# A hybrid attention layer on one core: attention buffers taken in order of release, two more buffers each for the stick-breaking weights, and their products with the values one unit later

## The chip, the cores and the metric

One core of one Trainium2 chip runs the whole layer. The metric is device time in microseconds. The kernel before takes 2918.4 us, the median of three runs (2916.21 to 2920.43). Names of engines follow the profile: PE is the matrix engine, PEld its weight load, DVE, ACT and POOL are the vector, scalar and general engines, SP is the engine that issues nearly all DMAs. Each engine works through its own instructions strictly in the order in which they were written.

## The reference, cut to what matters

Input and output are 2048 tokens by 1024 channels. One projection feeds two kinds of attention heads whose outputs are concatenated, projected and added; a SwiGLU feed-forward part follows.

```python
def stick_breaking_attention(q, k, v):          # 8 heads x 64
    ...
        z = jnp.einsum('bhqd,bhkd->bhqk', q[:, :, start:end], k[:, :, :end]).astype(jnp.float32) * scale
        log_beta = jax.nn.log_sigmoid(z)
        log_1m = jnp.where(past, jax.nn.log_sigmoid(-z), 0.0)
        acc = lax.cumsum(log_1m, axis=3, reverse=True) - log_1m
        w = jnp.where(past, jnp.exp(log_beta + acc), 0.0)
        outs.append(jnp.einsum('bhqk,bhkd->bhqd', w.astype(v.dtype), v[:, :, :end]))
    ...
def differential_attention(q, k, v, lam):       # 4 heads, two 64-wide q/k maps each
    ...
        p = jax.nn.softmax(jnp.where(causal, s, -jnp.inf), axis=-1)
        a = p[:, :, 0] - lam * p[:, :, 1]
        outs.append(jnp.einsum('bhqk,bhkd->bhqd', a.astype(v.dtype), v[:, :, :end]))
```

## The kernel before, in words

The program has four stretches: the first norm and projections, the stick-breaking heads in four groups of two heads (groups 0 to 3), the differential heads in four groups (4 to 7), and output projection and feed-forward. Every float32 product is done as three half-precision products, of a high part and a low part.

A group of stick-breaking heads is swept in *units*. A unit is one block of 128 queries (a = 0 or 1) against one piece of up to 512 keys, for both heads. Two units with the same keys, a = 0 and a = 1, make a *step*; a group has 20 steps, so there are 160 units in all. The sweep of a unit, `unit_sb`, is this:

- `scores` (PE): z = q k into PSUM. Two places in PSUM are used in turn, so the scores of unit u wait until DVE has read those of unit u-2.
- `main`: three sigmoids on ACT (L756 into `be`, L757 into `gp`, L758 within PSUM), two scans on DVE that form the running product (L761), a multiplication on DVE (L764), then on DVE the low part `wl` of the unit three back (L790, run by `clock.run("low")`), the carry from the step before (L769, or L767 where there is none), and a multiplication on POOL (L772).
- two units later `high` (ACT, L785): the high half `wh` of the weights; SP then issues a DMA that transposes it into `wt`.
- three units later `low` (DVE, L790): the low half `wl`, and its transposing DMA into a second `wt`.
- for a = 1, five units later `values` (PE): the transposed weights of the whole step, `wt`, times v.

The order is set by hand. `clock.at(d, fn, kind)` hangs work on the unit d units ahead; in each unit the loop over the plan runs the kinds "ev", "", main, "mid" and the rest in that order, then issues the scores of the unit after it, and then fills PE with projections of coming heads as long as PE's planned work is short of a goal. `values` has the kind "", so on PE it stands ahead of that unit's scores and filling. In many units there is nothing to fill with.

Buffers come from pools with a fixed number each: seven `pp` (L278) for `gp`, `be` and, in the other stretches, for input rows, normed rows and softmax weights; four `wh` (L281); four `wt` (L289, L780), two per step. Which buffer of a pool a new tile gets is the pool's choice when the program is built, and a write to it waits for the last reader of the tile that had it. Some of these choices fall on a buffer that was let go only lately: in group 1 tile `gp_4576` of unit 72 lies at the address of `be_4337` of unit 68, whose last reader is a `wl` that DVE runs in the unit just ahead (71). The room of the pools `csp`, `stp` and `rtp` is for the rotation of the differential heads' q and k; it is first written late in group 3.

Of the kernel before, what the change touches and what calls it, by code (L numbers as in the profile page):

```python
# [7 lines left out]
F32 = mybir.dt.float32  # L8
# [56 lines left out]
def hybrid_layer_kernel(  # L65
# [159 lines left out]
    with ExitStack() as actx:  # L225
        ac = actx.enter_context(tc.tile_pool(name="ac", bufs=1))
        OWN, NWT = (3,), 4
# [4 lines left out]
        csp = actx.enter_context(tc.tile_pool(name="csp", bufs=1))  # L232
        wtp = actx.enter_context(tc.tile_pool(name="wtp", bufs=NWT))
        stp = actx.enter_context(tc.tile_pool(name="stp", bufs=2))
        rtp = actx.enter_context(tc.tile_pool(name="rtp", bufs=1))
        onp = actx.enter_context(tc.tile_pool(name="onp", bufs=2))
        mxp = actx.enter_context(tc.tile_pool(name="mxp", bufs=2))
        psp = actx.enter_context(tc.tile_pool(name="psp", bufs=1, space=PSUM))
# [39 lines left out]
        def ptile(name):  # L278
            return ppp.tile([128, 1028], F32, tag="pp", name=name)

        def htile(name):  # L281
            return whp.tile([128, 1024], F16, tag="wh", name=name)

        wts = []

        def transposed(wh, w):

            if not wts:
                wt = wtp.tile([128, 2, 1024], F16, tag="wt", name="wt")  # L289
                wts.extend((wt[:, 0], wt[:, 1]))  # L290
            wt = wts.pop(0)[:, 0:w]
            nc.sync.dma_start_transpose(out=wt.rearrange("p (b q) -> p b q", q=128), in_=wh)
            return wt

        lam_t = rtp.tile([128, 1024], F32, tag="rt", name="lam_t")
# [267 lines left out]
        def project_diff(c, g):  # L563
# [10 lines left out]
            st = stp.tile([128, 2, 4, 2, 64], F32, tag="st", name="st")  # L574
# [43 lines left out]
            def squares():  # L618
                r["cs"] = csp.tile([128, 2, 4, 32], F32, tag="cs", name="cs")
# [3 lines left out]
                r["rt"] = rtp.tile([128, 1024], F32, tag="rt", name="rt")  # L623
# [87 lines left out]

        def units_sb(g):
# [7 lines left out]
        def unit_sb(g, s, c, a, cx, step):  # L720
# [27 lines left out]
            def main():  # L748


                z, sc = u["z"], scl[g]
                if a == 0:
                    step["gp"] = ptile("gp").rearrange("p (a h n) -> p a h n", a=2, h=2)
# [41 lines left out]
                if a == 1:  # L795
                    clock.at(5, values, "")
# [935 lines left out]
```

## Time and profile before

| | us |
|---|---|
| median of three runs | 2918.4 |
| the profiled execution: its time | 2919.95 |
| the profiled execution: its span | 2918.2 |
| busy in the span: PE, DVE, ACT, POOL | 2559.5, 2321.2, 1537.5, 1460.1 |
| groups 0 to 2 of the stick-breaking heads | 90 to 593 |
| group 3, and the turn to the differential heads | 593 to 815 |
| differential heads | 815 to 1506 |
| the rest of output projection, feed-forward | 1506 to 2918 |

The limits of the stretches were read from the times at which their lines first and last run, and are good to a unit or so. A row of a timeline is start, duration, engine, line, operation, what is written and read, and in brackets how long the engine had stood idle ahead of it and what ended that. A row of a table of waits is the waiting engine and line, what it waited for, and the microseconds in total, the number of times and the longest. A wait matters when the waiting engine is one on which the end depends; the chain of waits tells which those were.

### The profile page before, as it was taken

The page shows a single profiled execution, that of the slowest core. Times are in us where ns is not written, and L with a number is a line of the kernel's source. Part 1 is how long each engine was busy: PE and PEld are TensorE (multiplying, and loading weights), DVE is VectorE, ACT ScalarE, POOL GpSimd, SP SyncE. Part 2 cuts the span into 40 slices and gives each one's busy share as a digit, 9 for nine tenths or more (in the row PEclk, how much of TensorE's full clock was granted, in tenths as well). Part 3 has the DMA queues.
Part 4 walks back from the last instruction along what each step waited for, and adds up shares of the span by engine and source line. Part 5 has one row for each costly group of instructions (what it writes and reads, how often), then busy time and mean ns, then how long its engine had stood idle before and what let it go on. Part 6 is the DMA issues. An engine that isn't in the chain of part 4 may idle for free.

```text
span 2918.2 us, 50458 instructions
## 1 busy us (share of the span) xinstructions
PE 2559.5 (88%) x19628; PEld 1475.6 (51%) x19628; DVE 2321.2 (80%) x3639; ACT 1537.5 (53%) x2587; POOL 1460.1 (50%) x1131
## 2 busy tenths in 40 slices
PE   6868878888687787776998899999999999999999
PEld 4435444446576676665763344444444444444444
DVE  7787878878898899899747788889877776776776
ACT  5777777877555555555415454544443343343332
POOL 1344444546667577576115456555445454445442
PEclk9979989889798899988999999999999999999999
DMA  4466776776745565667866312221126422112111
GB/s 157 83 129 119 131 131 114 140 127 124 130 74 96 94 106 100 127 121 135 188 155 139 106 65 103 96 80 62 44 87 132 135 94 73 44 44 87 44 44 72
DMA packets 734240, 301.55 MB, mean 103 GB/s; under 512 B 618672, under 2 KB 713264, under 8 KB 734000
## 3 DMA queue, kind: packets, MB, share of 16 engines
q1 hardware_dynamic: 733856, 298.30, 45.6%
q8 instruction: 153, 2.51, 0.4%
q14 instruction: 87, 0.71, 0.1%
q0 software_dynamic: 144, 0.03, 0.0%
HBM read 127.34 MB, written 28.31 MB: 53 GB/s over the span
## 4 chain that ended last, share of the span: by engine, by line
PE 48%; DVE 22%; ACT 9%; DMA 7%; POOL 6%; issue 6%; SPq 1%; DVEq 0%; ACTq 0%; POOLq 0%
PE pw L167 33%; PE psum L167 15%; DMA wt<-wl 3%; DVE mx L178 2%; DVE fs L1316 2%; DVE wl L790 2%; DVE acc_a L1589 2%; DVE gp L761 2%; ACT be L756 2%; DVE pt L178 1%; ACT gp L757 1%; DVE hh L1368 1%; DVE be L764 1%; ACT wh L785 1%; ACT psum L758 1%
## 5 line engine op out<-in xcount | busy, mean ns | idle before, releaser
L167 PE MATMUL pw<-t,fs 128*128 128x512 f16 x3696 | 808.5, 381 | 13.3 <-ACT fs L1315 3.8
L167 PEld LDWEIGHTS <-fs 128*128 128x128 f16 x3696 | 360.5, 98 | 452.4 <-issue 13.9
L772 POOL TENSOR_TENSOR be<-be,gp 128x1024 f32<-128x1024 f32 (+1 forms) x160 | 323.1, 2019 | 363.6 <-DVE gp L769 177.7
L167 PE MATMUL pw<-acc_b,at 128*128 128x512 f16 x2112 | 465.5, 380 | 17.2 <-DVE cg L1514 6.3
L167 PE MATMUL psum<-k,q 64*128 64x512 f16 (+4 forms) x1600 | 293.0, 383 | 131.9 <-ACT pt L874 79.8
L167 PE MATMUL psum<-ws,h_hi 128*128 128x128 f16 x4096 | 378.9, 225 | 17.3 <-ACT psum L948 10.8
L167 PE MATMUL psum<-ws,h_lo 128*128 128x128 f16 x2048 | 367.7, 224 | 0.0
L167 PEld LDWEIGHTS <-h_hi 128*128 128x128 f16 x4096 | 328.8, 101 | 47.5 <-issue 35.4
L167 PEld LDWEIGHTS <-at 128*128 128x128 f16 x2112 | 206.1, 98 | 268.7 <-issue 24.9
L1517 POOL TENSOR_TENSOR cg<-cg,cu 128x512 f32<-128x512 f32 x88 | 111.9, 1272 | 360.9 <-ACT cg L1516 341.1
L1589 DVE SCALAR_TENSOR_TENSOR acc_a<-pw,isd,acc_a 128x512 f32<-128x512 f32 x352 | 248.6, 744 | 49.9 <-PE pw L167 49.5
L761 DVE TENSOR_TENSOR_SCAN gp<-gp,psum 128x256 f32<-128x256 f32 (+1 forms) x320 | 196.4, 655 | 114.8 <-ACT psum L758 112.9
L1315 ACT ACTIVATE fs<-acc_b,fst 128x512 f16<-128x512 f32 x264 | 175.9, 713 | 211.1 <-POOL acc_b L1304 145.1
L1316 DVE SCALAR_TENSOR_TENSOR fs<-acc_b,fst,fs 128x512 f16<-128x512 f32 x264 | 248.2, 980 | 34.0 <-ACT fs L1315 33.9
L1506 POOL TENSOR_TENSOR sc<-sc 128x512 f32<-128x512 f32 x132 | 219.3, 1678 | 88.9 <-ACT sc L1500 88.9
L167 PEld LDWEIGHTS <-q 64*128 64x128 f16 (+1 forms) x1600 | 95.8, 100 | 239.2 <-issue 116.4
L167 PE MATMUL psum<-wt,v 128*64 128x256 f16 x1728 | 138.8, 308 | 84.8 <-DMA wt<-wl 74.4
L1500 ACT COPY sc<-pw 128x512 f32<-128x512 f32 x176 | 100.1, 580 | 211.4 <-PE pw L167 185.2
L167 PEld LDWEIGHTS <-h_lo 128*128 128x128 f16 x2048 | 206.5, 101 | 0.0
L874 ACT ACTIVATE pt<-psum,nb,ds_sc 128x1024 f32<-128x1024 f32 (+4 forms) x192 | 182.8, 952 | 21.6 <-DVE pt L178 8.3
L178 DVE TENSOR_REDUCE mx<-psum 128x1 f32<-128x1024 f32 (+4 forms) x192 | 173.6, 904 | 22.3 <-PE psum L167 21.6
L790 DVE TENSOR_TENSOR wl<-be,wh 128x1024 f16<-128x1024 f32 (+1 forms) x160 | 186.8, 1168 | 0.9 <-DMA wt<-wl 0.8
(224 smaller groups left out, 4596.3 us busy)
## 6 DMA issues: line engine op xcount, KB each, us to landing
acc_b<-in_w_gate_dram SPq DMA_DIRECT2D x22, 1024.0 KB, 5.2
acc_b<-in_w_up_dram SPq DMA_DIRECT2D x22, 1024.0 KB, 7.5
acc_b<-in_w_down_dram SPq DMA_DIRECT2D x22, 1024.0 KB, 9.4
raw<-in_w_in_dram SPq DMA_DIRECT2D x24, 512.0 KB, 4.5
xt<-in_x_dram SPq DMA_DIRECT2D x16, 512.0 KB, 5.5
raw<-in_w_o_dram SPq DMA_DIRECT2D x16, 512.0 KB, 4.0
mt<-mix_d SPq DMA_DIRECT2D x32, 256.0 KB, 3.4
out_dram<-acc_a SPq DMA_DIRECT2D x16, 512.0 KB, 2.6
```

The costliest lines, as they stand in the source:

```text
L167: nc.tensor.matmul(ps, lhsT=lhsT, rhs=rhs, start=start, stop=stop)
L178: fn(*a, **k)
L761: nc.vector.tensor_tensor_scan(ga, ga, z[:, h, P:W][:, ::-1], 2.0 ** 14 if diag else cx[a][:, h, 0:1], ALU.mult, ALU.mult)
L772: nc.gpsimd.tensor_mul(b4, b4, gp[:, :, 1:P + 1].rearrange("p h (r n) -> p h r n", r=1).to_broadcast([128, 2, 2, P]))
L790: nc.vector.tensor_sub(wl, b2, u["wh"])
L874: nc.scalar.activation(pt, u["z"][:, 0:e - b], AF.Exp, scale=ds_sc, bias=nb[:, m:m + 1], accum_out=su[:, jj:jj + 1])
L1315: nc.scalar.activation(w[:, m, 0:4], src, AF.Copy, scale=sw)
L1316: nc.vector.scalar_tensor_tensor(w[:, m, 4:8], src, sw, w[:, m, 0:4], ALU.mult, ALU.subtract)
L1500: nc.scalar.copy(s[m], y[m])
L1506: nc.gpsimd.tensor_add(s[m], s[m], y[m])
L1517: nc.gpsimd.tensor_mul(g, g, u)
L1589: nc.vector.scalar_tensor_tensor(acc[:, i, hs], ps, pr.isd, acc[:, i, hs], ALU.mult, ALU.add)
```

## The change

Three things change, all in the attention part.

1. The pools of `pp`, `wh` and `wt` become rings: buffers made once, a list of the free ones in the order in which the program let them go, and a new tile takes the one that has been free longest (`take`, `give`). `gp` gets two `pp` buffers of its own, used in turn, for as long as the stick-breaking heads last; the other five serve `be`.
2. Two more `wh` and two more `wt` lie in the room of `csp`, `stp` and `rtp`. From the first unit of group 3 on they are taken only if nothing else is free, and `settle` gives the room over to the rotation when all four are free.
3. `values` runs six units after its step in groups 0 to 2. In group 3 it stays at five.

```diff
-        ppp = actx.enter_context(tc.tile_pool(name="ppp", bufs=7))
-        whp = actx.enter_context(tc.tile_pool(name="whp", bufs=4))
...
-        wtp = actx.enter_context(tc.tile_pool(name="wtp", bufs=NWT))
...
+        class Ring:
...
+            def __init__(self, name, n, shape, dt, pool=rgp):
+                self.all = [pool.tile(shape, dt, tag=f"{name}{i}", name=name) for i in range(n)]
+                self.free = list(self.all)
+                self.last = []
+
+            def take(self):
+                keep = [not any(t is l for l in self.last) for t in self.free]
+                return self.free.pop(keep.index(True) if True in keep else 0)
+
+            def give(self, t):
+                self.free.append(t)
+
+        pps = Ring("pp", 7, [128, 1028], F32)
+        whs = Ring("wh", 4, [128, 1024], F16)
+
+        wts = Ring("wt", 4, [128, 2, 1024], F16)
+
+        more_x = ExitStack()
+        mop = more_x.enter_context(tc.tile_pool(name="mop", bufs=1))
+        extra = [(ring, Ring(name, 2, shape, F16, mop).all)
+                 for ring, name, shape in ((whs, "wh", [128, 1024]), (wts, "wt", [128, 2, 1024]))]
+        for ring, tiles in extra:
+            ring.free.extend(tiles)
...
+        def settle():
+
+            if not pools:
+                if not all(any(t is f for f in ring.free) for ring, tiles in extra for t in tiles):
+                    return False
+                for ring, tiles in extra:
+                    ring.free = [f for f in ring.free if not any(t is f for t in tiles)]
+                more_x.close()
+                for name, bufs in (("csp", 1), ("stp", 2), ("rtp", 1)):
+                    pools[name] = actx.enter_context(tc.tile_pool(name=name, bufs=bufs))
+            return True
+
+        def retire():
+
+            for ring, tiles in extra:
+                ring.last = tiles
...
+            while not settle():
+                yield END
             while staged[0] == 2:
                 yield END
...
+                if not gps:
+                    gps.extend((pps.take(), pps.take()))
                 if a == 0:
-                    step["gp"] = ptile("gp").rearrange("p (a h n) -> p a h n", a=2, h=2)
-                gp = step["gp"][:, a]
-                be = ptile("be")[:, 0:2 * W].rearrange("p (h n) -> p h n", h=2)
+                    gps.reverse()
+                if g == SBP - 1 and s == 0:
+                    retire()
+                gp = gps[0].rearrange("p (a h n) -> p a h n", a=2, h=2)[:, a]
+                bt = pps.take()
+                be = bt[:, 0:2 * W].rearrange("p (h n) -> p h n", h=2)
...
                 def high():
-                    wh = u["wh"] = htile("wh")[:, 0:n]
-                    nc.scalar.copy(wh, b2)
-                    turned(wh, 0)
+                    wh = u["wh"] = whs.take()
+                    nc.scalar.copy(wh[:, 0:n], b2)
+                    turned(wh[:, 0:n], 0)
 
                 def low():
-                    wl = htile("wl")[:, 0:n]
-                    nc.vector.tensor_sub(wl, b2, u["wh"])
-                    turned(wl, 1)
+                    wl = whs.take()
+                    nc.vector.tensor_sub(wl[:, 0:n], b2, u["wh"][:, 0:n])
+                    turned(wl[:, 0:n], 1)
+                    whs.give(u["wh"])
+                    whs.give(wl)
+                    pps.give(bt)
...
                 if a == 1:
-                    clock.at(5, values, "")
+                    clock.at(6 if g < SBP - 1 else 5, values, "")
...
+                for y in range(2):
+                    wts.give(step[y])
                 if c == 0:
                     clock.at(2, store, "")
```

The input rows, the softmax weights and the weight halves of the differential heads take and give back in the same way; a `pp` tile of the first softmax map goes back when the two maps are mixed, the other when its low part is formed.

What the built programs then hold, at two places. The first is ACT in group 1, two steps without a diagonal, before and then after (`pp_124` and `pp_127` are the two `gp` buffers now, the other `pp` are `be`; the old names carry a number of their own for each tile). What an instruction waits for stands in brackets, by engine or DMA lane.

```order
L756 ACTIVATE be_4577<-psum_122,gsc_137 128x1024 [waits PE_49]
L757 ACTIVATE gp_4576<-psum_122,gsc_137 128x2x256 [waits DVE_49]
L758 ACTIVATE psum_122<-psum_122,gsc_137 128x2x256 [waits Activation_49]
L785 CAST wh_4589<-be_4438 128x1024 [waits DMAHW1_49,Pool_49]
L756 ACTIVATE be_4625<-psum_122,gsc_137 128x1024 [waits DVE_49,PE_49]
L757 ACTIVATE gp_4576<-psum_122,gsc_137 128x2x256
```

```order
L802 ACTIVATE pp_126<-psum_107,gsc_122 128x1024 [waits DVE_49,PE_49]
L803 ACTIVATE pp_127<-psum_107,gsc_122 128x2x256 [waits DVE_49]
L804 ACTIVATE psum_107<-psum_107,gsc_122 128x2x256 [waits Activation_49]
L831 CAST wh_132<-pp_125 128x1024 [waits DMAHW7_49,Pool_49]
L802 ACTIVATE pp_129<-psum_107,gsc_122 128x1024 [waits DVE_49,PE_49]
L803 ACTIVATE pp_127<-psum_107,gsc_122 128x2x256 [waits DVE_49]
```

Both write `gp` after a wait for DVE, but for another instruction: before, for L790 in the unit just ahead; now for L815 (the carry, old L769) two units back. The wait of `be` for DVE now stands in most units, and is for L836 (the low part, old L790) that DVE runs two units back.

The second place is SP in group 1, the transposing DMAs of two steps, before and then after.

```order
L781 DMA_TRANSPOSE wt_5722<-wh_5720 128x8x128 [waits DMAHW5_49,DMAHW7_49,PE_49,Activation_49]
L781 DMA_TRANSPOSE wt_5787<-wl_5785 128x8x128 [waits DMAHW6_49,DVE_49,PE_49]
L781 DMA_TRANSPOSE wt_5722<-wh_5791 128x8x128 [waits Activation_49]
L781 DMA_TRANSPOSE wt_5787<-wl_5873 128x8x128 [waits DMAHW0_49,DVE_49]
L781 DMA_TRANSPOSE wt_5882<-wh_5880 128x8x128 [waits DMAHW2_49,DMAHW1_49,DMAHW4_49,PE_49,Activation_49]
```

```order
L827 DMA_TRANSPOSE wt_143<-wh_132 128x8x128 [waits DMAHW5_49,PE_49,Activation_49]
L827 DMA_TRANSPOSE wt_144<-wh_133 128x8x128 [waits DMAHW6_49,DVE_49]
L827 DMA_TRANSPOSE wt_143<-wh_141 128x8x128 [waits DMAHW7_49,Activation_49]
L827 DMA_TRANSPOSE wt_144<-wh_142 128x8x128 [waits DMAHW0_49,DVE_49]
L827 DMA_TRANSPOSE wt_134<-wh_130 128x8x128 [waits DMAHW1_49,PE_49,Activation_49]
```

The number and order of the DMAs stay, apart from the stores of results (`mix_d`), which move with `values`. The first DMA of a step waits for PE before and now, but three steps instead of two lie between two uses of a `wt`, and three units instead of two between two uses of a `wh`. On PE the products with the values move behind one more unit's scores and filling; the rest of PE's order is the same but for single pieces of filling.

More of the change, by code (lines that the diff above doesn't have):

```diff
@@ L293, in transposed @@
+        def retire():
+            for ring, tiles in extra:
+                ring.last = tiles
+        halves_free = []
+        def transposed(wh, w):
+            if not halves_free:
+                t = wts.take()
+                halves_free.extend((t[:, 0], t[:, 1]))
+            wt = halves_free.pop(0)
+            nc.sync.dma_start_transpose(
+                out=wt[:, 0:w].rearrange("p (b q) -> p b q", q=128), in_=wh)
             return wt
-        lam_t = rtp.tile([128, 1024], F32, tag="rt", name="lam_t")
+        lam_t = whs.free[-1].bitcast(F32)
@@ L872, in main @@
                                          scale=nds_sc, bias=lnk)
-                pt = ptile("pt")[:, 0:e - b]
+                while gps:
+                    pps.give(gps.pop())
+                cx["t", m, j] = pps.take()
+                pt = cx["t", m, j][:, 0:e - b]
                 nc.scalar.activation(pt, u["z"][:, 0:e - b], AF.Exp, scale=ds_sc,
@@ L908, in mix @@
                 big(nc.vector.scalar_tensor_tensor, p0, p1, cx["cf"][:, 1:2], p0, ALU.mult, ALU.add)
+                pps.give(cx["t", 1, jc])
             def high(jc):
@@ L912, in high @@
                 w = p0.shape[-1]
-                wh = cx["wh", jc] = htile("ah")[:, 0:w]
+                cx["th", jc] = whs.take()
+                wh = cx["wh", jc] = cx["th", jc][:, 0:w]
                 if n == 2:
@@ L922, in low @@
                 w = p0.shape[-1]
-                wl = htile("al")[:, 0:w]
+                tl = whs.take()
+                wl = tl[:, 0:w]
                 if jc == 0 and n == 2:
@@ L928, in low @@
                 cx["wt", jc].append(transposed(wl, w))
+                for ring, t in ((whs, cx["th", jc]), (whs, tl), (pps, cx["t", 0, jc])):
+                    ring.give(t)
             def values():
@@ L1057, in tick @@
             clock.step()
-        g1 = stp.tile([128, D], F32, tag="st", name="g1")
+        g1 = flat(wts.free[-1]).bitcast(F32)
         xts = {}
         def load_x(i):
-            xts[i] = ptile("xt")[:, 0:D]
-            nc.sync.dma_start(out=xts[i], in_=xr[i])
+            xts[i] = pps.take()
+            nc.sync.dma_start(out=xts[i][:, 0:D], in_=xr[i])
         nc.sync.dma_start(out=g1, in_=attn_norm_g.to_broadcast([128, D]))
@@ L1084, in norm_in, with turn_in @@
         def norm_in(i):
[L1085 to L1091 removed]
+            pt, rs = hns.pop(i)
+            xt, hn = xts.pop(i), pt[:, 0:D]
+            big(nc.vector.scalar_tensor_tensor, hn, xt[:, 0:D], rs, g1, ALU.mult, ALU.mult)
+            pps.give(xt)
+            def turn_in():
+                transpose_split(hn, h_hi, h_lo, i, place, "z", ident)
+                pps.give(pt)
+            clock.at(1, turn_in)
         for i in range(NT + 2):
@@ L1103, in hybrid_layer_kernel @@
             if i < NT:
-                hn = ptile("hn")[:, 0:D]
-                hns[i] = hn, norm_rstd(xts[i], hn)
+                hn = pps.take()
+                hns[i] = hn, norm_rstd(xts[i][:, 0:D], hn[:, 0:D])
                 if 3 < i + 3 < NT:
```

42 lines of the change are left out of this document (14 added, 28 removed).

## The prediction

> **What bounds the kernel now.** First the table of stretches (columns: busy time and count of PE, PEld, DVE, ACT, POOL, then granted clock, DMA share, GB/s), cut where the change cuts: groups 0 to 2 with the later products, group 3 without, differential heads, the rest.
>
> ```profile
> core 0: us, PE busy (x) PEld busy (x) DVE busy (x) ACT busy (x) POOL busy (x), PEclk, DMA share, GB/s
> 90.00:593.00 503.00, 404.53 (x3732) 225.47 (x3729) 406.82 (x725) 389.48 (x535) 235.28 (x116) 0.88 0.68 125
> 593.00:815.00 222.00, 173.39 (x2073) 122.54 (x2072) 189.25 (x322) 151.41 (x224) 134.02 (x82) 0.90 0.66 122
> 815.00:1506.00 691.00, 553.09 (x6775) 466.77 (x6774) 590.02 (x1004) 369.56 (x890) 406.35 (x409) 0.92 0.63 120
> 1506.00:2918.00 1412.00, 1364.76 (x6579) 617.43 (x6579) 1076.52 (x1489) 577.55 (x869) 667.85 (x486) 0.99 0.27 83
> ```
>
> In groups 0 to 2 no engine is full: PE and DVE are busy 80% and 81% of the time, ACT 77%. About 100 us pass in which each of them waits, so this stretch is bound by waits between engines. Which ones, the chain of waits of this stretch tells:
>
> ```profile
> by line: PE psum L167 35.2%; DMA wt<-wl 11.8%; issue 8.4%; ACT be L756 6.8%; DVE gp L761 6.7%; DVE wl L790 6.1%; ACT gp L757 5.4%; ACT wh L785 4.0%; ACT psum L758 4.0%; DVE be L764 4.0%; DMA wt<-wh 2.8%; DVE ws L161 1.4%; SPq L781 0.7%; ACT
> ```
>
> The transposing DMAs of the weights hold 14.6% of it, 73 of 503 us, though they are no engine's work. The table of waits for the same stretch names who stands still (total, times, longest):
>
> ```profile
> DVE gp L761 <- ACT psum L758: 93.0, 79, 3.1
> PE psum L167 <- DMA wt<-wl: 53.6, 29, 3.6
> PE psum L167 <- DVE be L764: 32.1, 19, 3.4
> ACT gp L757 <- DVE wl L790: 29.9, 26, 2.3
> ACT wh L785 <- DMA wt<-wh: 16.9, 19, 2.4
> PE psum L167 <- DMA wt<-wh: 8.0, 11, 1.8
> ```
>
> Nearly all of DVE's idle time (503 - 407 = 96 us) is its wait for ACT's last sigmoid, so ACT is late, and ACT is late because of its own waits or because scores come late. How one hangs on the other is seen in one step of group 1 with nothing to fill PE:
>
> ```profile
> 406.66 0.30 PE L167 MATMUL psum<-wt,v 128*64 128x256 f16 x2
> 407.02 1.23 SPq L781 DMA_TRANSPOSE wt<-wl  x1
> 410.34 2.56 PE L167 MATMUL psum<-wt,v 128*64 128x256 f16 x22 [3.38 <-DMA wt<-wl]
> 411.82 0.69 ACT L757 ACTIVATE gp<-psum,gsc 128x512 f32<-128x512 f32 x1 [2.25 <-DVE wl L790]
> 412.54 0.66 ACT L758 ACTIVATE psum<-psum,gsc 128x512 f32<-128x512 f32 x1
> 412.83 1.46 PE L167 MATMUL psum<-k,q 64*128 64x512 f16 x6
> 413.24 1.39 DVE L761 TENSOR_TENSOR_SCAN gp<-gp,psum 128x256 f32<-128x256 f32 x2 [1.38 <-ACT psum L758]
> 414.36 1.11 ACT L756 ACTIVATE be<-psum,gsc 128x1024 f32<-128x1024 f32 x1 [0.20 <-PE psum L167]
> 419.68 2.56 PE L167 MATMUL psum<-wt,v 128*64 128x256 f16 x22 [3.02 <-DMA wt<-wl]
> ```
>
> Two loops. PE reaches the products with the values 3.38 us before their low half has landed; the next scores stand behind them in PE's order, and ACT's `be` behind those. And ACT, with `be` done, may not write `gp` until DVE has ended an unrelated `wl`; DVE then stands idle 1.38 us while ACT does the two short sigmoids that DVE needs. The step takes 419.68 - 410.34 = 9.34 us.
>
> **What a step needs.** Means of the large forms over all four groups:
>
> ```profile
> L761 DVE TENSOR_TENSOR_SCAN gp<-gp,psum 128x256 f32<-128x256 f32 x256 | 173.2, 718 | 96.0 <-ACT psum L758 94.1 <-PE psum L167 1.4
> L790 DVE TENSOR_TENSOR wl<-be,wh 128x1024 f16<-128x1024 f32 x128 | 162.5, 1270 | 0.3 <-DMA wt<-wl 0.2
> L764 DVE TENSOR_TENSOR be<-be,psum 128x512 f32<-128x512 f32 x128 | 84.7, 662 | 0.0
> L785 ACT CAST wh<-be 128x1024 f16<-128x1024 f32 x128 | 133.2, 1040 | 40.9 <-DMA wt<-wh 18.4 <-DVE gp L769 12.9 <-DVE gp L767 5.0
> L757 ACT ACTIVATE gp<-psum,gsc 128x512 f32<-128x512 f32 x127 | 87.1, 686 | 29.9 <-DVE wl L790 29.7
> L758 ACT ACTIVATE psum<-psum,gsc 128x512 f32<-128x512 f32 x127 | 84.1, 662 | 4.1
> ```
>
> A unit costs DVE 2 x 0.718 + 0.662 + 1.270 = 3.37 us and the small carry, ACT 1.11 + 0.686 + 0.662 + 1.040 = 3.50. A step cannot be shorter than about 7.0 us, so even the step above could give at most 9.34 - 7.0 = 2.3 of its 3.3 us of waiting (3.02 and a little for `wh`): seven tenths. Steps with PE filled give less.
>
> **The change part by part.** No arithmetic and no DMA is added or removed; the sum has only waits.
>
> *Products one unit later, with the six `wt` that this needs.* The move puts a unit (3.5 us or more) between landing and use. The landing itself is from the view of this tile (least, median, most):
>
> ```profile
> DMA to landing us min/median/max: 2.4/3.2/5.0
> ```
>
> So waits of 1.85 us in the mean (53.6 / 29) vanish, but for a rest after the slowest landings. PE waits 53.6 + 8.0 = 61.6 us here. Bounds: nothing, if the next wait on the chain is already as long; all 61.6 if all of it passes through. From the step above the most is seven tenths; steps whose neighbours fill PE pass less. I take a half: **31 us**. Group 3 keeps five units and its PE waits of 20.9 us, at no gain.
>
> ```profile
> PE psum L167 <- DMA wt<-wl: 20.9, 15, 3.7
> ACT gp L757 <- DVE wl L790: 12.8, 7, 4.6
> ```
>
> *`gp` with buffers of its own.* Its wait is now for a carry two units back, which is past when ACT gets there, in all four groups. It was 29.9 us in groups 0 to 2, largely in the same steps as the waits above, so that only a quarter is counted on top: 7. In group 3, where the products stay, half of 12.8: 6. Together **13 us**; bounds 0 and 42.7.
>
> *Six `wh`.* ACT's wait of 16.9 us for the transpose two units back (three now) goes; it lies behind the same late DMAs, so I count **2 us**, bounds 0 and 16.9. The SP queue is freed of its own waits for PE at a step's first DMA, which brings landings forward, not back:
>
> ```profile
> SPq L781 <- PE psum L167: 31.0, 30, 2.3
> ```
>
> *What is new.* `be` must now wait in most units for the `wl` that DVE runs right behind the multiplication on which the scores wait as well:
>
> ```profile
> 405.19 0.66 DVE L764 TENSOR_TENSOR be<-be,psum 128x512 f32<-128x512 f32 x1
> 405.77 1.22 DVE L790 TENSOR_TENSOR wl<-be,wh 128x1024 f16<-128x1024 f32 x1
> 405.91 0.82 PE L167 MATMUL psum<-k,q 64*128 64x512 f16 x6 [0.98 <-DVE be L764]
> ```
>
> `wl` ends at 406.99, the scores at 406.73: 0.26 us, covered here since ACT began that `be` only at 408.45. Without cover it is 0.26 us in up to 80 even units, 21 us. Denser work also sets DVE and POOL against each other:
>
> ```profile
> 429.45 2.36 POOL L772 TENSOR_TENSOR be<-be,gp 128x1024 f32<-128x1024 f32 x1 [2.81 <-DVE gp L769]
> 431.20 1.70 DVE L790 TENSOR_TENSOR wl<-be,wh 128x1024 f16<-128x1024 f32 x1
> ```
>
> This `wl` took 1.70 us instead of 1.22, with 0.61 us of it beside POOL's multiplication: 0.48 lost. If DVE runs units back to back, `wl` starts 2.1 us after the carry (scans and multiplication), and POOL, started by that carry, runs up to 2.36: 0.2 to 0.3 us lost per unit. For both together I take **-10 us**, bounds 0 and -50. The Trainium skill, "SBUF — State Buffer", section "SBUF: two separate sides", says that these two engines share one pair of ports as an exclusive lock, and that the later one stands still until the first is done. By that rule the whole overlap would be lost, 0.61 instead of the 0.48 that this row shows, and the 10 us would be 13; it is the one rule that speaks against the change.
>
> *The other stretches.* At the start, ACT waits for input rows only at the first loads, and in the differential heads the waits of `pt` for a buffer let go in the same unit are small, in a stretch where DVE is busy 85%:
>
> ```profile
> ACT pt L874 <- DVE pt L178: 8.3, 11, 1.1
> ACT pt L874 <- POOL al L925: 5.4, 3, 2.1
> ACT hn L188 <- DMA xt<-in_x_dram: 5.4, 2, 5.2
> ```
>
> I count 0, bounds -5 (a worse choice of buffers somewhere) and +10. The hand-over of the two extra pairs costs nothing: they are last taken at the beginning of group 3, and the rotation first writes there some 17 units later.
>
> Sum: -31 - 13 - 2 + 10 = -36 us. From the profiled execution's own 2919.95 us (span 2918.2; 1.5 us above the median of the runs) that is **2884 us**.
>
> **The rivals.**
>
> *All of it passes through.* For: the idle time of DVE and PE in these steps is one and the same event, and ending the pauses spares PE its slow restarts: the 22 products took 2.56 us after a pause of 3.38, where the row below has 24 in 1.50 without a pause.
>
> ```profile
> 436.56 1.50 PE L167 MATMUL psum<-wt,v 128*64 128x256 f16 x24
> ```
>
> DVE at 90% in groups 0 to 2 would need 407 / 0.9 = 452 us, 51 fewer; with 10 in group 3 and the differential heads, 2859 us. The Trainium skill, "TensorE: Matmul & The Clock Gate", section "What's actually happening", gives PE half its clock after an idle window of about 3.4 us; by it a pause of 3 us need not always cost this, as the window runs free. The rows agree with the halving.
>
> *The waits only change their names.* For: 32.1 us of PE waiting for DVE and 93 us of DVE waiting for ACT stand beside the DMA's; three engines near 80% leave little slack to each. The DMA wait turns into one of these, and the time stays within 0.2% (6 us; less than that a measurement of this kernel cannot tell from no change): 2917 us. Against: in the step shown each of them is downstream of the two that go.
>
> *Ports.* DVE gets denser, and loses 0.3 us in each of 120 units of groups 0 to 2 to POOL: 36 us, the whole gain: 2920 us.
>
> *Slower: `be` behind `wl`.* Before, only `gp` waited for a `wl`, with the 1.11 us of `be` already done. If ACT now meets an unfinished `wl` already at `be`, that 1.11 us falls behind it as well. In 33 places (26 and 7) this eats 37 us, the gain; above that the change is a loss, and with 52 places 2884 + 58 = 2942 us. Against: that `wl` is a unit older than the one that held `gp`.
>
> **How the numbers follow.** Forecast 0.55 (own range 2865 to 2903, from a third to three quarters of the waits); all through 0.18; names only 0.13; ports 0.05; slower 0.09. The likeliest gives 2884 us. Leaving out the lower half of "all through" and the slower case gives the range 2852 to 2918. Faster: 0.55 + 0.18 + some of the ports' case = 0.75; the same 0.15; slower 0.10.
>
> **What would show it.** Right: PE's wait for `wt` under 15 us in groups 0 to 2 and still about 20 in group 3; no wait of `gp` for a `wl`; DVE's wait for ACT down to some 60 us; groups 0 to 2 in about 470 us; the stretches behind them unchanged within 5 us. Wrong: `be` waiting for `wl` by more than 10 us, the mean of `wl` above 1.4 us, or groups 0 to 2 still at 500 us with DVE waiting for ACT as before.

## The result, and the profile after

The changed kernel takes 2872.3 us, the median of four runs (2869.6 to 2877.5), beside 2919.4 us (2916.2 to 2923.5) for the kernel before: a ratio of 0.984, 95% interval 0.982 to 0.986. The prediction was 2884 us, so the sign was right; the gain of 47 us is 11 us larger than the 36 us that were forecast. The profiled execution took 2869.62 us, its span is 2867.8.

Where the time went is read from the first `be` of each group and the last of all:

| first `be` to first `be`, us | before | after | gained |
|---|---|---|---|
| group 0 | 173.2 | 156.0 | 17.2 |
| group 1 | 170.4 | 158.2 | 12.2 |
| group 2 | 169.1 | 153.2 | 16.0 |
| group 3 (to the last `be`) | 192.7 | 192.8 | -0.1 |
| from there to the end of the span | 2129.4 | 2124.6 | 4.8 |

Groups 0 to 2 gave 45 of the 50 us between the two profiled executions. Group 3 gave nothing. The 4.8 us behind the last `be` are no clear gain: in the profiled executions of all the kernels here that stretch takes 2122 to 2132 us, with code that is the same but for the choice of buffers.

The table of stretches of the changed kernel, cut at the same places (columns: busy time and count of PE, PEld, DVE, ACT, POOL, then granted clock, DMA share, GB/s):

```profile
90.00:547.00 457.00, 383.41 (x3720) 219.23 (x3719) 415.44 (x722) 384.46 (x533) 235.46 (x116) 0.93 0.76 137
547.00:770.00 223.00, 174.15 (x2088) 122.92 (x2084) 193.93 (x327) 151.47 (x226) 136.07 (x84) 0.90 0.68 123
770.00:1460.00 690.00, 557.90 (x6783) 468.72 (x6782) 589.93 (x1003) 370.11 (x889) 406.00 (x409) 0.91 0.62 120
1460.00:2868.00 1408.00, 1362.72 (x6573) 617.13 (x6571) 1075.65 (x1489) 577.50 (x869) 668.51 (x486) 0.99 0.27 83
```

In groups 0 to 2 DVE is busy 91% of the time instead of 81%, with 9 us more of busy time (415 against 407). PE did as many products (3720 records against 3732) in 383.4 us instead of 404.5, and its granted clock rose from 0.88 to 0.93. So of the 46 us by which this stretch became shorter, PE's idle time gave 25 (98.5 to 73.6) and PE's own running time 21. How a pause slows PE is seen in the kernel before, in two stretches that follow each other (columns as above):

```profile
425.08:428.49 3.41, 0.78 (x14) 0.61 (x14) 2.38 (x4) 2.52 (x4) 1.56 (x1) 1.00 0.81 157
428.49:431.90 3.41, 3.05 (x29) 1.62 (x25) 2.45 (x6) 2.62 (x5) 2.36 (x1) 0.50 0.53 115
```

PE was busy for 0.78 us in the first, which holds a pause of 2.63 us, and the granted clock is 0.50 all through the second. The Trainium skill, "TensorE: Matmul & The Clock Gate", section "What's actually happening", has half the clock after an idle window of about 3.4 us that runs free. The trace agrees with the halving and with a window of that length, but the window need not be wholly idle: 0.78 us of work in it did not prevent the half clock.

The waits of groups 0 to 2 after (total, times, longest):

```profile
PE psum L167 <- DVE pp L810: 58.0, 39, 5.5
DVE pp L807 <- ACT psum L804: 39.2, 30, 4.6
PE psum L167 <- DMA wt<-wh: 7.7, 7, 3.0
ACT wh L831 <- DMA wt<-wh: 3.6, 4, 1.4
```

PE's 61.6 us of waiting for the transposes are 7.7 now, DVE's 93.0 for ACT are 39.2, and the wait of `gp` (now L803) for a low half has no row any more. Nor has `be` (L802) a row for a wait for a low half (L836); four waits of `be`, 1.3 us in all, are put down to the carry right behind one (L815). What grew is PE's wait for DVE's multiplication (L810), from 32.1 to 58.0: PE is now the one that is early.

A unit of group 1 without filling, from the timeline of ACT and DVE:

```profile
387.26 1.12 ACT L802 ACTIVATE pp<-psum,gsc 128x1024 f32<-128x1024 f32 x1
387.74 0.66 DVE L810 TENSOR_TENSOR pp<-pp,psum 128x512 f32<-128x512 f32 x1
388.27 0.69 ACT L803 ACTIVATE pp<-psum,gsc 128x512 f32<-128x512 f32 x1
388.31 1.22 DVE L836 TENSOR_TENSOR wh<-pp,wh 128x1024 f16<-128x1024 f32 x1
388.99 0.66 ACT L804 ACTIVATE psum<-psum,gsc 128x512 f32<-128x512 f32 x1
389.45 0.15 DVE L815 TENSOR_REDUCE pp<-pp 128x2 f32<-128x2 f32 x1
389.57 1.03 ACT L831 CAST wh<-pp 128x1024 f16<-128x1024 f32 x1
389.68 1.39 DVE L807 TENSOR_TENSOR_SCAN pp<-pp,psum 128x256 f32<-128x256 f32 x2
390.51 1.12 ACT L802 ACTIVATE pp<-psum,gsc 128x1024 f32<-128x1024 f32 x1
390.98 0.66 DVE L810 TENSOR_TENSOR pp<-pp,psum 128x512 f32<-128x512 f32 x1
```

From `be` to `be` 3.25 us, from multiplication to multiplication 3.24 us, and no row has a bracket: both engines run without a gap. Two such units take 6.5 us, less than the 7.0 us that the prediction took for the least a step can have: a row begins up to 0.1 us before the row ahead of it on its engine ends (`gp` begins at 388.27, `be` ends at 388.38), so the sum of the rows is more than the time that they need. Before, the step that the prediction shows took 9.34 us.

Group 3, with products at five units before and after: the cast's wait for the transposes before, then two waits after.

```profile
ACT wh L785 <- DMA wt<-wh: 9.0, 9, 2.9
```

```profile
PE psum L167 <- DMA wt<-wh: 20.5, 16, 3.4
ACT wh L831 <- DMA wt<-wh: 18.5, 14, 3.2
```

The 12.8 us that `gp` waited there are gone, PE's 20.5 us for the transposes are what they were (20.9), and the cast to the high half waits 18.5 us for transposes that it waited 9.0 for before. The group takes as long as before, so what left one wait came back in others.

### The profile page after: what moved, and what is told of

It reads as the page before. It is cut to its first block, busy times and chain, and to the rows that moved or that the text cites. A ratio compares the mean times of both kernels' runs of the same rounds, so it can differ in the third digit from the quotient of the medians.

```text
span 2867.8 us, 50589 instructions
## 1 busy us (share of the span) xinstructions
PE 2540.9 (89%) x19628; PEld 1470.6 (51%) x19628; DVE 2333.7 (81%) x3639; ACT 1533.4 (53%) x2587; POOL 1462.7 (51%) x1131
## 4 chain that ended last, share of the span: by engine, by line
PE 43%; DVE 20%; ACT 6%; POOL 5%; DMA 5%; issue 5%; SPq 1%; DVEq 0%; POOLq 0%; ACTq 0%
PE pw L167 33%; PE psum L167 10%; DMA wt<-wh 2%; DVE mx L178 2%; DVE fs L1382 2%; DVE acc_a L1655 2%; DVE pp L178 1%; DVE hh L1434 1%; DVE pp L807 1%; DVE wh L836 1%; DMA q<-rt 1%; DVE wmx L105 1%; DVE rt L683 1%; DVE st L675 1%; ACT pp L802 1%
## 5 line engine op out<-in xcount | busy, mean ns | idle before, releaser
L818 POOL TENSOR_TENSOR pp<-pp 128x1024 f32<-128x1024 f32 (+1 forms) x160 | 325.1, 2032 | 316.2 <-DVE pp L815 139.8
L807 DVE TENSOR_TENSOR_SCAN pp<-pp,psum 128x256 f32<-128x256 f32 (+1 forms) x320 | 195.9, 653 | 56.0 <-ACT psum L804 55.1
L836 DVE TENSOR_TENSOR wh<-pp,wh 128x1024 f16<-128x1024 f32 (+1 forms) x160 | 204.7, 1279 | 0.3 <-DMA wt<-wh 0.3
L931 ACT ACTIVATE pp<-psum,nb,ds_sc 128x1024 f32<-128x1024 f32 (+4 forms) x192 | 183.0, 954 | 22.8 <-DVE pp L178 8.6
L802 ACT ACTIVATE pp<-psum,gsc 128x1024 f32<-128x1024 f32 (+1 forms) x160 | 164.8, 1030 | 34.5 <-PE psum L167 30.5
```

The source lines that it names most:

```text
L802: nc.scalar.activation(be, z[:, :, 0:W], AF.Sigmoid, scale=sc[:, 0:1])
L807: nc.vector.tensor_tensor_scan(ga, ga, z[:, h, P:W][:, ::-1], 2.0 ** 14 if diag else cx[a][:, h, 0:1], ALU.mult, ALU.mult)
L818: nc.gpsimd.tensor_mul(b4, b4, gp[:, :, 1:P + 1].rearrange("p h (r n) -> p h r n", r=1).to_broadcast([128, 2, 2, P]))
L836: nc.vector.tensor_sub(wl[:, 0:n], b2, u["wh"][:, 0:n])
L931: nc.scalar.activation(pt, u["z"][:, 0:e - b], AF.Exp, scale=ds_sc, bias=nb[:, m:m + 1], accum_out=su[:, jj:jj + 1])
```

## Experiments

Ratios are to the kernel before on the same chip; "groups" are the times of groups 0, 1 and 2 by first `be`, beside 173.2, 170.4, 169.1 before and 156.0, 158.2, 153.2 after. The changed kernel itself, by its ratio, is 47 us faster than before. A difference of two such figures is good to some 6 or 7 us.

### The parts of the change

**Products at five units everywhere, all else as changed.**

```diff
-                    clock.at(6 if g < SBP - 1 else 5, values, "")
+                    clock.at(5, values, "")
```

> The changed kernel with the products with the values five units after their step in all groups; the rings and the extra buffers stay. Theory of the waits (the gain of 47 us comes mostly from PE no longer waiting for the transposed weights): that wait returns in groups 0 to 2, from 7.7 us to some 50, and about 28 us of the gain are lost: 2900 us. Rival, buffers alone (order of release and two more of each are what pays): at most 5 us are lost, 2872 to 2877 us.

Measured: 2906.4 us, ratio 0.994 (0.992 to 0.995); groups 169.1, 171.2, 164.2.

```profile
PE psum L167 <- DMA wt<-wh: 59.2, 45, 3.1
```

```profile
90.00:584.00 494.00, 398.14 (x3725) 224.11 (x3722) 414.98 (x722) 385.10 (x533) 233.73 (x116) 0.91 0.71 127
```

Without the later products PE waits 59.2 us for the transposes again, in more and shorter waits than before (45 against 40), and only 18 of 47 us are gained: some 28 are lost, as the theory of the waits expected. PE's busy time (second fence, the stretch of groups 0 to 2) is 398.1 us, between the 404.5 before and the 383.4 after.

**The same with no extra buffers.**

```diff
-        extra = [(ring, Ring(name, 2, shape, F16, mop).all)
-                 for ring, name, shape in ((whs, "wh", [128, 1024]), (wts, "wt", [128, 2, 1024]))]
+        extra = []
```

> The changed kernel without the extra buffers and with the products at five units: rings in order of release and the two gp buffers alone. Theory of the waits: only ACT's wait of gp for wl is gone (42.6 us of waiting), 8 to 15 us faster than the kernel before: 2904 to 2911 us, with PE's wait for the weights at 55 us or more in groups 0 to 2. Buffers alone: 2880 us or less. A third possibility, that the order is worth nothing without the later products: 2917 us.

Measured: 2912.6 us, ratio 0.996 (0.9945 to 0.9975); groups 172.1, 170.7, 164.6.

```profile
PE psum L167 <- DMA wt<-wh: 63.3, 45, 3.1
ACT wh L830 <- DMA wt<-wh: 32.2, 30, 3.2
```

The order of release and `gp`'s own pair give 12 us by themselves, within the 8 to 15 that were expected. With four `wh` the cast waits 32.2 us for a transpose two units back; before it was 16.9.

**Products at six units and six `wt`, but four `wh`.**

```diff
-                 for ring, name, shape in ((whs, "wh", [128, 1024]), (wts, "wt", [128, 2, 1024]))]
+                 for ring, name, shape in ((wts, "wt", [128, 2, 1024]),)]
```

> The changed kernel with only the two extra wt; wh stays at four. Theory: ACT's wait of wh for its transpose comes back (some 15 us in groups 0 to 2) but is mostly covered: 2872 to 2880 us. Rival, the wh are what frees ACT: 2885 us or more.

Measured: 2896.9 us, ratio 0.990 (0.989 to 0.992); groups 165.3, 169.3, 160.2.

```profile
DVE pp L807 <- ACT psum L804: 61.5, 52, 4.4
ACT wh L831 <- DMA wt<-wh: 37.6, 39, 2.8
PE psum L167 <- DMA wt<-wh: 6.7, 5, 3.1
```

PE no longer waits for the transposes, but ACT's cast waits 37.6 us for the same transposes, and DVE 61.5 us for ACT. The two extra `wh`, to which the prediction gave 2 us, are worth 0.0064 of 2921, 19 us. That is the rival's side: the wait is not covered.

Together, in us against before, from the ratios: rings alone -12; with both extra pairs -18; with later products and four `wh` -28; with everything -47. The later products are worth 16 with four `wh` and 28 with six; the `wh` pair 7 with early products (beside the idle extra `wt`) and 19 with late ones. The two belong together: each lifts a wait for one and the same DMA on another engine.

**`gp` out of the common ring of seven.** Everything else as changed.

```diff
-                if not gps:
-                    gps.extend((pps.take(), pps.take()))
                 if a == 0:
-                    gps.reverse()
+                    gps.append(pps.take())
...
-                gp = gps[0].rearrange("p (a h n) -> p a h n", a=2, h=2)[:, a]
+                gp = gps[-1].rearrange("p (a h n) -> p a h n", a=2, h=2)[:, a]
...
+                if a == 1 and len(gps) > 1:
+                    pps.give(gps.pop(0))
```

> The changed kernel, but gp takes the longest free of the seven pp like be does, and is given back when the next step has read it; no buffers of its own. Theory: order of release is enough to keep gp away from a wl just ahead, so no change: 2868 to 2878 us, and no wait of gp for wl above 3 us. Rival, the two buffers of its own are needed: that wait returns with 20 us or more and the time is 2880 us or more.

Measured: 2948.9 us, ratio 1.008 (1.006 to 1.009): slower than before; groups 180.0, 177.9, 180.2.

```profile
DVE pp L805 <- ACT psum L802: 122.3, 72, 5.2
ACT pp L800 <- DVE pp L813: 70.5, 31, 3.5
```

Here `be` (L800) waits 70.5 us behind DVE, and 29.5 us more in a row that names L811 in place of L813. The names are those of the carry, but what `be` waits for is the low half (L834) right ahead of the carry on DVE:

```profile
311.15 1.22 DVE L834 TENSOR_TENSOR wh<-pp,wh 128x1024 f16<-128x1024 f32 x1
312.46 0.69 ACT L800 ACTIVATE pp<-psum,gsc 128x512 f32<-128x512 f32 x1 [2.27 <-DVE pp L813]
```

The low half ends at 312.37 and `be` begins 0.09 us later. In all 50 of these waits `be` begins 0.09 to 0.10 us behind the end of a low half, while its distance from the carry varies (0.03 or 0.08 us). All fall on units with a = 0. There `gp` takes the oldest free buffer and `be` the next, which is the one that a low half let go in the unit just ahead; the program has `be` wait for that low half. This is the prediction's slower rival itself, `be` behind `wl`. `gp` has no wait for a low half, as the theory expected, but `be` got it. In this ring order of release is no cure; the reserved pair is, and it makes 70 us of difference (2949 against some 2879 on this chip).

**A unit later still.**

```diff
-                    clock.at(6 if g < SBP - 1 else 5, values, "")
+                    clock.at(7 if g < SBP - 1 else 5, values, "")
```

> The changed kernel with the products seven units after their step in groups 0 to 2. Theory that DVE is the bound of these groups now (91% busy): no gain from one unit more, 2868 to 2876 us, though PE's wait for the weights (7.7 us) falls to about 0; with six wt the first transpose of a step may wait for PE as it did before. Rival, PE's wait still sets the time: 2865 us or less.

Measured: 2872.8 us, ratio 0.984 (0.982 to 0.985); groups 161.9, 151.5, 150.0. In this kernel the last sums of group 2 and the second of group 3 fall into one place of PSUM, so that the result of the last 256 queries of group 2 is lost; number and kind of the instructions are the same, so the time can still be read for what one unit more would give.

PE's wait for the transposes has no row left, and no time is gained outside the interval. What was to be had from lateness is had with six.

**Group 3 at six units too.** Its products were to come six units later in its first nine steps, with no buffers added, to see whether PE's 20.5 us there are what holds it. There is no time for this: the ring of `wt` has no free buffer when a high half asks for one. Whether group 3 would gain from later products is not known.

### Which engine sets the time now

**Added work on DVE, in the changed kernel and in the kernel before.** One reduction more per unit of groups 0 to 2, whose result is not used.

```diff
                 clock.run("low")
+                if g < SBP - 1:
+                    nc.vector.reduce_max(small("dum", bufs=2), be[:, 0, 0:W], axis=AX.X)
```

> The changed kernel with one more DVE instruction per unit in groups 0 to 2, a maximum over 512 (or 256) numbers whose result nobody uses: 120 of them, an estimate of 0.3 to 0.6 us each from the 0.904 us of a maximum over 1024, so about 55 us of DVE work. If DVE is the bound now, nearly all of it shows: +45 to +55 us. If the groups are still bound by waits of other engines, half: +25 to +30 us.

> The same added DVE work in the kernel before. Theory that it was bound by waits: part of the work falls into DVE's idle 96 us, and +20 to +40 us show, clearly fewer than in the changed kernel. Rival, DVE was the bound there as well: as many as in the changed kernel.

Measured: 2917.9 us in the changed kernel (ratio 0.9986, 0.998 to 1.000) and 2940.3 in the kernel before (1.0066, 1.005 to 1.009). The groups by form (count, then busy us and mean ns), first of the changed kernel, then of the one before:

```profile
L813 DVE TENSOR_REDUCE dum<-pp 128x1 f32<-128x512 f32 x93 | 62.8, 675 | 0.0
L813 DVE TENSOR_REDUCE dum<-pp 128x1 f32<-128x256 f32 x22 | 9.0, 407 | 0.0
```

```profile
L767 DVE TENSOR_REDUCE dum<-be 128x1 f32<-128x512 f32 x94 | 63.7, 678 | 0.0
L767 DVE TENSOR_REDUCE dum<-be 128x1 f32<-128x256 f32 x22 | 9.0, 407 | 0.0
```

Of 71.8 us added to the changed kernel 43 show (0.0146 of 2921), 59%; of 72.7 added before, 19, 26%. By the intervals each of the two is good to some 7 us, and they differ by more. The added work was more than the 55 us expected, because the 0.904 us behind that estimate is a mean over several lengths, and the 675 ns shown is what 512 numbers take. By its share the 59% lies between the two theories, nearer to the half that was to show if other engines' waits bind than to nearly all. So DVE is not the bound alone, but added work shows on it more than before, and PE pays too: its busy time in the stretch is 396.5 us instead of 383.4. The obvious conclusion, that taking work from DVE would pay, was then tried, and falls.

**Every fourth, and every second, low half on POOL.**

```diff
-                    nc.vector.tensor_sub(wl[:, 0:n], b2, u["wh"][:, 0:n])
+                    lows[0] += 1
+                    eng = nc.gpsimd if g < SBP - 1 and lows[0] % 4 == 0 else nc.vector
+                    eng.tensor_sub(wl[:, 0:n], b2, u["wh"][:, 0:n])
```

> The changed kernel, but in groups 0 to 2 every fourth subtraction that makes a low half of the weights runs on POOL instead of DVE, at the same place in the program. Theory (DVE's load is what bounds groups 0 to 2 now, and POOL, 51% busy there, has room): some 30 subtractions of 1.3 us leave DVE, 39 us; with the 0.59 that added work on DVE showed, 23 us less, from which ports and a subtraction that may be twice as long on POOL take half: 2860 us (2850 to 2868). Rival (ACT's 3.5 us per unit, or the loop between scores and multiplication, is as short a bound as DVE): no change, 2872 within 4. Rival (a low half that ends later on POOL holds back `be` and the products): 2880 or more.

> As the run with every fourth, with every second subtraction on POOL. Theory: 60 subtractions leave DVE, 78 us; DVE falls to some 75% and is no longer the bound, and POOL at 2.2 us for each multiplication and some 2.5 for each subtraction comes to 365 us of 457, 80%: at best another 10 us gained over every fourth. Rival (the two engines stand on each other's ports): the multiplication on POOL and DVE's scans grow by as much as is saved, and the time is that of the changed kernel or above, 2872 to 2890.

Measured: 2871.2 us (ratio 0.983, 0.9805 to 0.985) and 2870.6 (0.983, 0.981 to 0.985): the time of the changed kernel. First the stretch of groups 0 to 2 and the low halves with every fourth, then with every second:

```profile
90.00:543.00 453.00, 384.77 (x3721) 220.63 (x3722) 385.04 (x692) 384.23 (x533) 295.31 (x144) 0.93 0.75 138
L839 DVE TENSOR_TENSOR wh<-pp,wh 128x1024 f16<-128x1024 f32 x63 | 95.1, 1510 | 0.0
L839 POOL TENSOR_TENSOR wh<-pp,wh 128x1024 f16<-128x1024 f32 x29 | 61.9, 2134 | 0.0
```

```profile
90.00:546.00 456.00, 384.17 (x3702) 220.29 (x3701) 361.24 (x663) 384.12 (x532) 350.89 (x172) 0.92 0.76 137
L839 DVE TENSOR_TENSOR wh<-pp,wh 128x1024 f16<-128x1024 f32 x46 | 80.0, 1739 | 0.0
```

DVE's share fell from 91% to 85% and 79%, and the stretch is as long as before. Two things are seen. The low halves that stay on DVE grow, 1406 to 1510 and 1739 ns in groups 0 to 2, so that of 78 us meant to leave DVE 54 left it (415.4 to 361.2). And DVE's freed time does not shorten the stretch, but turns into waiting for ACT, 83.9 us instead of 39.2 with every second low half on POOL:

```profile
DVE pp L808 <- ACT psum L805: 83.9, 69, 6.2
```

Two pieces of four units each show it, one of group 1 with little filling and one of group 2 with much; first the changed kernel, then every second low half on POOL:

```profile
281.37:294.15 12.78, 9.89 (x87) 4.76 (x86) 12.78 (x22) 11.78 (x19) 6.59 (x5) 1.00 0.94 180
517.85:533.60 15.75, 14.70 (x194) 10.40 (x192) 14.93 (x25) 14.22 (x20) 9.30 (x5) 1.00 0.91 147
```

```profile
283.86:297.33 13.47, 11.63 (x94) 5.41 (x93) 11.77 (x22) 11.70 (x20) 12.18 (x7) 1.00 0.85 180
516.77:532.56 15.79, 14.70 (x194) 10.40 (x192) 13.45 (x23) 14.22 (x19) 13.24 (x7) 1.00 0.83 148
```

In the changed kernel DVE fills the first piece wholly, but ACT fills 92% of it. With DVE down to 87% the piece is no shorter (13.47 us); POOL is at 90% there now. In the second PE, DVE and ACT are at 93, 95 and 90%; with DVE at 85% the piece still takes 15.8 us. So DVE was not the bound by itself: one or two other engines are at 90% or more in the same units. That they alone hold the time is not shown. Some of the gain may have been lost to the later low halves: with every second on POOL, PE waits 18.6 us for transposes (7.7 in the changed kernel) and `be` 9 us for a subtraction on POOL. Group by group the result differs, too: group 0 is 5 us longer than in the changed kernel and group 1 5 us shorter. The rival of the ports is not borne out as it was put: the multiplication on POOL (2240 ns) and the scans on DVE (718) are as long as before; only the low halves on DVE grew.

**Added work on ACT.** In groups 0 to 2 the first half of the cast to the high half is done twice; the result is the same.

```diff
+                    if g < SBP - 1:
+                        nc.scalar.copy(wh[:, 0:n // 2], b2[:, 0:n // 2])
                     nc.scalar.copy(wh[:, 0:n], b2)
```

> The changed kernel with added work on ACT: in groups 0 to 2 the first half of each cast to the high half is done twice (0.61 us for the large form, 0.4 for the small, some 65 us in all; the result is the same). Theory (ACT is as near a bound as DVE): at least half of it shows, as the 0.59 for DVE's added work, 2872 + 33 to 2872 + 50. Rival (DVE alone is near its limit, ACT has 16% of idle room): a quarter or less, below 2872 + 17.

Measured: 2898.1 us, ratio 0.992 (0.991 to 0.994), 25 us slower than the changed kernel by the ratios.

```profile
L832 ACT CAST wh<-pp 128x512 f16<-128x512 f32 x93 | 56.8, 611 | 0.9 <-POOL pp L818 0.8
L832 ACT CAST wh<-pp 128x256 f16<-128x256 f32 x23 | 9.2, 398 | 0.0
```

Of 66.0 us added 25 show, 37%. That lies between what the two theories expected (half or more, a quarter or less): ACT has more slack than DVE, but it is near.

**Both relieved: every second low half on POOL, every third cast from ACT to DVE.**

```diff
-                    nc.scalar.copy(wh[:, 0:n], b2)
+                    lows[1] += 1
+                    if g < SBP - 1 and lows[1] % 3 == 0:
+                        nc.vector.tensor_copy(wh[:, 0:n], b2)
+                    else:
+                        nc.scalar.copy(wh[:, 0:n], b2)
```

> The changed kernel with every second low half on POOL, as in the run before, and in groups 0 to 2 every third high half (the cast, 1.04 us) on DVE instead of ACT. Theory (ACT, at 3.5 us per unit, is as near a bound as DVE was, and what left DVE could not show for that reason): 38 casts leave ACT, 38 us with the short ones; with all three engines below 3.3 us per unit the gain is 10 to 20 us, 2852 to 2862. Rival (the loop of scores, sigmoids, scans and multiplication, some 6 us for the two places in PSUM, or PE with its fillings sets the time): no change, 2868 to 2875. Rival (the cast in DVE's order stands behind the carry and waits for POOL's multiplication, which now comes later): slower, 2880 or more.

Measured: 2882.8 us, ratio 0.987 (0.986 to 0.989): 9 us slower than the changed kernel.

```profile
L836 ACT CAST wh<-pp 128x1024 f16<-128x1024 f32 x62 | 64.4, 1039 | 9.7 <-POOL pp L819 9.1 <-DMA wt<-wh 0.6
L834 DVE CAST wh<-pp 128x1024 f16<-128x1024 f32 x30 | 41.6, 1388 | 0.0
```

```profile
ACT pp L803 <- POOL wh L843: 23.7, 19, 2.6
PE psum L167 <- DMA wt<-wh: 22.7, 16, 3.6
```

ACT's casts fell, but the cast costs 1.39 us on DVE against 1.04 on ACT. ACT's `be` (L803 here) now waits 23.7 us for a subtraction on POOL, which lets a buffer go later than DVE did, and PE waits 22.7 us for transposes again, which fits low halves that land later. The rival that named 2880 or more gave another reason, a cast on DVE that waits for POOL's multiplication; the casts on DVE show no idle time (0.0). Neither relief reaches the end. Whether a division exists that relieves both engines without delaying a low half was not found.

### Ports

**The low half behind the carry instead of ahead of it.** On DVE only the order of two instructions changes.

```diff
-                clock.run("low")
                 if diag:
                     nc.vector.memset(gp[:, :, P:P + 1], 2.0 ** 14)
                 else:
                     nc.vector.tensor_reduce(gp[:, :, P], cx[a][:, :, 0:1], axis=AX.X, op=ALU.max)
+                clock.run("low")
```

> The changed kernel with the low part wl behind the carry on DVE instead of ahead of it, in all units: POOL's multiplication starts 1.2 us earlier and runs beside wl. If the two engines stand in each other's way, as the 1.70 us row of the kernel before suggests, the mean of wl rises from 1.38 us to 1.9 or more, and the time by 20 to 60 us. If they do not, wl stays at 1.4 us and the time falls by up to 10 us, since POOL and all behind it are earlier.

Measured: 2872.7 us, ratio 0.984 (0.982 to 0.986), no different from the changed kernel. POOL's multiplication and the low half in groups 0 to 2 (busy us and mean ns, then idle time ahead), first with the low half behind the carry, then of the changed kernel, last the low half of the kernel before:

```profile
L818 POOL TENSOR_TENSOR pp<-pp 128x1024 f32<-128x1024 f32 x94 | 270.9, 2885 | 137.7 <-DVE pp L814 87.8 <-DVE pp L812 19.6 <-ACT ws L157 9.6
L836 DVE TENSOR_TENSOR wh<-pp,wh 128x1024 f16<-128x1024 f32 x91 | 118.6, 1303 | 0.0
```

```profile
L818 POOL TENSOR_TENSOR pp<-pp 128x1024 f32<-128x1024 f32 x94 | 210.3, 2237 | 191.1 <-DVE pp L815 108.4 <-DVE pp L813 43.2 <-ACT psum L804 18.1
L836 DVE TENSOR_TENSOR wh<-pp,wh 128x1024 f16<-128x1024 f32 x91 | 127.9, 1406 | 0.0
```

```profile
L790 DVE TENSOR_TENSOR wl<-be,wh 128x1024 f16<-128x1024 f32 x92 | 117.1, 1273 | 0.2 <-DMA wt<-wl 0.2
```

With the carry first, POOL and DVE set out together, and it is POOL that loses, 2885 ns a multiplication instead of 2237, while the low half gets shorter, 1303 instead of 1406. POOL, 51% busy there in the changed kernel, has the room. The Trainium skill, "SBUF — State Buffer", section "SBUF: two separate sides", has the two engines hold a shared pair of ports in turn, whichever starts first keeping it for its whole instruction; the rows agree in that the loser can be either engine. POOL lost 0.65 us in the mean, half of a low half's 1.30.

## Why the prediction was right, and where its numbers were not

The mechanism was right in the main: a gain, made in groups 0 to 2, by the waits it named; but one of them, the cast's, it had put near nothing. The gain came to 46 us in this stretch, where the prediction's "about 470 us" meant 33, and to nothing in group 3, where it meant 6. That 2884 lies as near to the result as it does is in part luck: 10 us for a cost that cannot be found in the time and 2 us for `wh` were too cautious, 6 us in group 3 were too many.

- **Products one unit later, "I take a half: 31 us".** The later products alone gave 16 us, and 28 us together with six `wh`. The half was nearly right for the pair, but its reasoning counted PE's idle time alone. Of the 46 us, 21 are PE's busy time, at a granted clock of 0.93 instead of 0.88. The prediction had this effect only in its rival "all of it passes through". The ceiling of seven tenths does not hold either: it rests on 7.0 us for a step, and two units of the changed kernel take 6.5.
- **Six `wh`, "I count 2 us".** This is the term that was mis-sized. It measured some 19 us with the later products, 7 without, each good to some 6; its upper bound was 16.9. The row behind the bound was ACT's wait for the transposes in the kernel before. With four `wh` and `gp`'s wait gone the cast waits 32.2 us for them, and 37.6 with the later products. A bound taken from a wait of the old kernel does not hold where other parts of the change let the waiting engine arrive earlier.
- **`gp` with buffers of its own, 13 us.** Rings and `gp`'s pair alone measured 12 us, but the agreement is luck. In the profiled execution with these alone groups 0 to 2 are 5 us shorter, where 7 were counted, and group 3, given 6, is 2 us longer; the rest lies behind the last `be`, where executions differ by as much. In the changed kernel the wait of 12.8 us in group 3 went as forecast, and the cast's wait grew in its place.
- **`be` behind `wl`, and ports, "-10 us".** In groups 0 to 2 `be` waits for a low half for 1.3 us at most, so that part cost next to nothing; the kernel with `gp` in the common ring shows that it can cost the whole gain. The ports' part is there in busy time: the large low half rose from 1273 to 1406 ns, the small from 775 to 921, some 15 us over this stretch, and DVE's busy time by 9. Whether it cost time is open: with the carry first the low halves are shorter (1303 ns) and nothing is faster, but there POOL's multiplications are longer instead.
- **Other stretches, 0 (-5 to +10).** Measured -4.8 us behind the last `be`, within what executions of these kernels differ by there. In the differential heads the times of the groups of waits are the same within a few us, so the order of release did nothing that can be seen there.

Of what the prediction asked for: PE's wait for `wt` under 15 us (7.7) and about 20 in group 3 (20.5), no wait of `gp` for a low half, the stretches behind unchanged within 5 us, all as asked. DVE's wait for ACT came to 39 instead of some 60 us, and groups 0 to 2 to 457 instead of 470. On the other side, the mean of `wl` reached 1406 ns, which is the 1.4 us named there as a sign of being wrong; the gain came all the same.

Of the rivals, "all of it passes through" (2859 us) named the second half of the mechanism, DVE at 90% and PE without its slow restarts, and asked for 51 us in groups 0 to 2, of which 45 came; 2872 lies halfway between it and the forecast. "The waits only change their names" is true of group 3, and in part of the kernel with four `wh`, which gained 28 of the 47 us. "Slower: `be` behind `wl`" did not happen here, but is what the kernel with `gp` in the common ring does: 23 us slower than before.

Why it stops at 2872 us is shown in part. DVE and ACT run gapless in the unit shown, and PE is at 93% in the piece with filling. Work added to DVE shows by 59%, to ACT by 37%; work taken from DVE alone shows by nothing. Whether it is full engines or later low halves that ate what was taken from DVE, and what a perfect balance would give, stays open.

## What to carry to other kernels

Ask of each wait for a DMA which engines meet the same landing: here PE (products) and ACT (the buffer of the cast) stood behind one transpose, and of the 35 us beyond the rings freeing PE alone gave 16 and freeing ACT alone 7. A ring in order of release helps only if every tile finds a buffer that is really old: when `gp` took the oldest one, `be` was left with the one let go in the unit just ahead. With so few free, count for each tile which buffer it gets and when its last reader runs. Read a wait's name against the times, too: the row named the carry, and the distance from the low half told what it was. That added work shows on an engine does not mean that removed work will: look whether a second engine is full in the same units before moving work.

## What the runs showed of the hardware that was not expected

- PE's products became cheaper by 21 us (404.5 to 383.4 us for the same work) as its pauses became shorter; with the products at five units and all else as changed it was 398. In the kernel before, a pause of 2.63 us was followed by 3.41 us at half the granted clock.
- DVE and POOL take time from each other in both directions. As POOL did more, DVE's subtraction rose from 1406 to 1510 and 1739 ns; when DVE's subtraction came behind the carry, POOL's multiplication rose from 2237 to 2885 ns. The Trainium skill, "Perfetto Trace Analysis", section "Optimizing Scalar/DVE Operations", warns that moving work between these two may not help for this reason; here 54 of 78 us did leave DVE, and the time stayed all the same, with DVE waiting 45 us more for ACT.
- The same cast took 1388 ns on DVE and 1039 on ACT, and the same subtraction 2134 ns on POOL, beside 1273 on DVE in groups 0 to 2 of the kernel before.
